# Sixteen experts taken in pairs of 64 places each, with their weights used in plain fp32 as they were loaded

## The chip, the core and the metric

The kernel runs on one core of one Trainium2 chip. The metric is the device time of one execution in microseconds (us); less is better. An execution is one launch with all of its inputs in HBM.

## What is computed

Two transformer blocks run one after the other on 256 tokens of width 1024, everything in float32. The first block is a gated mixer of three branches, a cross attention to 256 memory rows, and a hierarchical mixture of experts; the second is attention with a gated scan, a second cross attention, and a feed-forward layer with a short convolution. Only the mixture of experts changes here:

```python
def hierarchical_moe(h, w_rg, b_rg, w_re, b_re, w_e_gate, w_e_up, w_e_down):
    t = h.reshape(-1, d)                                   # 256 x 1024
    p_grp = softmax(t @ w_rg + b_rg)                       # 4 groups
    g_val, g_idx = top_k(p_grp, 1)
    le = (t @ w_re + b_re).reshape(n, 4, 4)                # 4 experts in each group
    p_exp = softmax(take_along_axis(le, g_idx))
    e_val, e_idx = top_k(p_exp, 2)                         # two experts for a token, of one group
    weight = g_val * e_val / sum(e_val)
    gate = sum(one_hot(g_idx * 4 + e_idx, 16) * weight)    # 256 x 16
    act = silu(t @ w_e_gate[e]) * (t @ w_e_up[e])          # 16 experts, each 1024 -> 256
    return sum over e of (act * gate[:, e]) @ w_e_down[e]  # 256 -> 1024
```

An expert has 2 MiB of gate and up weights and 1 MiB of down weights; the sixteen have 50.3 MB.

## The kernel before

The program is one stream of instructions whose order a planner writes when the kernel is built. Its class `Net` keeps a clock of every engine by a table of costs (`Clock`, `Engine`, `mm`), and small tasks (`spawn`, `advance`, `run`, `need`) are put in where this clock says that their inputs are there.

All weights are one stream, `wstream`, in the order of `PLAN`, cut into pieces of 512 KB (128 partitions by 1024 numbers, `weight_plan`, lines 36 to 108). An expert is six pieces, four of gate and up and two of down. `load` (line 484) issues the DMA of the next piece as soon as a buffer is free: six buffers `stg`, and further ones that `lend` (line 501) takes from the general tiles `t8`, four pieces from before the mixture of experts on (`EARLY`, line 1687) and four more from the experts' loop on (`LEND`, line 1556). They show in the trace as `t<-wstream`.

The precision comes from three F32R matmuls: `split_weight` (line 459) makes of each piece a rounded copy `whi` on ScalarE and the rest `wlo` on VectorE, four and three buffers of a piece each, and the activations are split in the same way. `take` hands out both parts. `mm` (line 659) puts 1 cycle a column on the planner's clock for a matmul of the type F32R, and 4 for plain F32.

The mixture of experts (`moe`, line 1475) goes so. `route` finds for each token its group and counts its rank in the group; `sel` is a 0/1 matrix of 256 tokens by 4 groups by 128 places. While `fill` still computes keys for the second block, `xtok` turns the tokens round, `gathers` collects them by `sel` into 4 x 128 places, split into `xgh` and `xgl`; `scalars` collects the factors of each place and `selt` turns `sel` round. Then all engines read the largest count and pass a branch (line 1552): `overflow` computes what found no place, and it is skipped where no group has more than 128 tokens. A hint for the branch stands in line 1539. `experts` (line 1560) then runs the sixteen experts: for each, 8 chunks by 3 matmuls of 512 columns (`up_mm`), the gated activation (`expert_hidden`: ScalarE, VectorE, two transposes, a split into `mea`), and 2 chunks by 2 halves by 3 matmuls (`down_mm`). The up part of the next expert stands ahead of the down part of this one. All 128 places of a group go through its four experts; after the fourth, `combine` copies the sum from PSUM, splits it, and takes the places back to tokens by 16 matmuls of 256 columns. Then `between` (line 1694) adds the result and begins the second block, whose first weights follow in the stream.

Of the kernel before, what the change touches and what calls it, by code (L numbers as in the profile page):

```python
# [35 lines left out]
def weight_plan():  # L36
# [37 lines left out]
    def gate_up(e):  # L74
        for k in range(0, 8, 2):
            plan.append(("w_e_gu", e, np.arange(k * P, (k + 2) * P), np.arange(512)))

    gate_up(0)
    for e in range(16):
        if e < 15:  # L80
            gate_up(e + 1)
        for k in range(2):
            plan.append(("w_e_down", e, np.arange(k * P, (k + 1) * P), np.arange(1024)))
# [27 lines left out]
PLAN = weight_plan()  # L111

# [158 lines left out]
class Net:  # L271
    BANKS, MORE = 4, 6
    HI, LO, STG = 4, 3, 6
    EARLY, LEND, BACK = 2, 2, 14
# [9 lines left out]
    def __init__(self, ctx, tc, aps, dbg=None):  # L284
# [29 lines left out]
        self.ringed, self.spare, self.lent, self.lending = set(), [], {}, False  # L314

# [115 lines left out]
    def splits(self, margin=None):  # L431

        c, f = self.c, self.c.free
        for n, eng, lim, tag in ((self.n_lo, "dve", self.LO - 1, ("wlo", self.LO)),
# [17 lines left out]

    def room(self, tag, bufs):

        ring = self.rings.get((id(self.wsp), tag), [])
        kept = {x.tensor.name for x in self.kept[tag].values()}
        return 0.0 if len(ring) < bufs else min((self.c.used(x) for x in ring if x not in kept), default=0.0)

    def split_weight(self, eng, n, src):
# [6 lines left out]
        else:  # L466
# [4 lines left out]
            del self.stage[n], src  # L471
            self.ringed.discard(n)
            if n in self.lent:
                view = self.lent.pop(n)
                if self.lending:
                    self.spare.append(view)
            self.load()
# [23 lines left out]
    def lend(self, n):  # L501

        self.lending = True
        for _ in range(n):
            t = self.t8().rearrange("p a t -> p (a t)")
            self.spare += [t[:, :1024], t[:, 1024:]]
        self.load()
# [52 lines left out]
    def force(self):  # L560

        n, eng = (self.n_lo, "dve") if self.n_lo < self.n_hi else (self.n_hi, "act")
# [82 lines left out]

    def block(self, act, k):
# [12 lines left out]
    def mm(self, out, lhsT, rhs, start, stop):  # L659
        n = size(rhs)  # L660
        slow = rhs.dtype == F32
        self.c.issue("pe", max(0.107 if slow else 0.027, 0.0022 + n * (4 if slow else 1) / 2400.0), [lhsT, rhs], [out])
# [301 lines left out]
    def consts(self):  # L964
# [26 lines left out]
        self.iota = c[:, 768:896]  # L991
# [300 lines left out]
    def route(self, rc, sel):  # L1292
# [15 lines left out]
        yield PE  # L1308
        rkp = bank[:, 64:72].rearrange("p (i g) -> p i g", i=2)
        cnt = bank[:, 72:76]  # L1310
        self.mm(rkp[:, 0], self.tri, ohg[:, 0], False, True)
        self.mm(rkp[:, 1], self.ones, ohg[:, 0], False, False)
        self.mm(rkp[:, 1], self.tri, ohg[:, 1], False, True)
        for i in range(2):
            self.mm(cnt, self.ones, ohg[:, i], False, i == 1)
# [14 lines left out]
        rm, rk = self.pc(4), self.pc(1)  # L1330
        V.tensor_mul(rm, rkp, ohg)
        V.tensor_reduce(rk, rm, axis=AX.X, op=ALU.add)
        for g in range(4):
            for i in range(2):
                V.tensor_scalar(sel[:, i, g], self.iota, rk[:, i], ohg[:, i, g:g + 1],
                                op0=ALU.is_equal, op1=ALU.mult)
        self.routed = (ohg, rk)
        yield
# [5 lines left out]
        l2 = self.pc(4)  # L1344
        V.scalar_tensor_tensor(l2, oh1, -3.0e38, ls, op0=ALU.mult, op1=ALU.add)
        _, oh2 = self.first_max(l2)
        V.tensor_add(oh1, oh1, oh2)
# [4 lines left out]
        sv = self.col(16).rearrange("p (i e) -> p i e", i=2)  # L1352
        V.tensor_copy(sv[:, :, 0:1], rc[:, :, None])
        V.tensor_mul(sv[:, :, 1:5], ex, b4(s2))
        self.sv = sv

    def slot_scalars(self, out, bank, sels):

        n = len(sels)
        b = bank[:, :8 * n].rearrange("p (g e) -> p g e", g=n)[:, :, 0:5]  # L1360
        for g, sel in enumerate(sels):
            for i in range(2):
                self.mm(b[:, g], sel[:, i].bitcast(F32), self.sv[:, i, 0:5], i == 0 and g == 0, i == 1)
        self.V.tensor_copy(out[:, :, 0:5], b)
        self.V.tensor_mul(out[:, :, 1:5], out[:, :, 1:5], out[:, :, 0:1].to_broadcast([P, n, 4]))

    def expert_hidden(self, h, sc, e, ea):

        s = self.tile(self.ph[0], [P, T], F32, "hs", 2)
        self.S.activation(s, h[:, 0:T], AF.Silu, scale=sc[:, 0:1])  # L1370
        self.V.scalar_tensor_tensor(s, h[:, T:2 * T], sc[:, 1 + e:2 + e], s, op0=ALU.mult, op1=ALU.mult)
# [4 lines left out]
        hv = h[:, :T].rearrange("p (j t) -> p j t", j=2)  # L1376
        self.S.copy(ea[0], hv)
        self.V.tensor_sub(ea[1], hv, ea[0])

    def new_ea(self, bufs=4):  # L1380
        return [self.tile(self.ph[0], [P, 2, P], F32R, "mea", bufs) for _ in range(2)]

    def up_mm(self, h, xh, xl, wb, k, nk=8):
        for whi, wlo in wb:
            self.mm(h, xh[:, k], whi, k == 0, False)
            self.mm(h, xh[:, k], wlo, False, False)
            self.mm(h, xl[:, k], whi, False, k == nk - 1)
            k += 1
        return k

# [1128 lines left out]
```

## Time and profile before

| | |
|---|---|
| median of 3 runs | 951.21 us (949.74 to 951.82) |
| the profiled execution's own time | 953.05 us |
| its span, first to last instruction | 951.2 us |
| TensorE busy | 924.7 us (97%), 6288 matmul instructions |
| TensorE weight loads | 853.9 us (90%) |
| VectorE busy | 747.1 us (79%) |
| ScalarE busy | 597.7 us (63%) |
| HBM read | 177.72 MB, mean with the rest 188 GB/s over the span |

The profile is that of one execution. Matmuls are pipelined: the duration that a row shows for one contains its way through the array, so what a matmul costs in a stream is read from the distance between two starts and not from its duration. Nearly all instructions were recorded by two helpers, line 266 for VectorE and ScalarE and lines 663 and 667 for TensorE matmuls and transposes, so that groups are told apart by the names of their tiles. A plain fp32 matmul shows as two instructions, each with its own weight load. The stage of the experts begins at 359.04 us and ends at 506.00 us.

### The profile page before, as it was taken

How to read it: one execution, taken by the hardware profiler on the slowest of the kernel's cores; microseconds unless marked ns; L12 is line 12 of the kernel's file. 1: busy time of each engine (PE TensorE's matmuls, PEld its weight loads, DVE VectorE, ACT ScalarE, POOL GpSimd, SP SyncE). 2: the span in 40 equal slices, each digit the busy share in tenths (PEclk: the TensorE clock that was granted, in tenths of full speed). 3: DMA queues.
4: the chain of work that ended last, by engine and by line, in shares of the span. 5: the costliest groups of instructions: out<-in, count | busy, mean ns of one | idle time of the engine just before them, and what ended most of it. 6: DMA issues, size and time to landing. Idle time of an engine off the chain costs nothing.

```text
span 951.2 us, 16270 instructions
## 1 busy us (share of the span) xinstructions
PE 924.7 (97%) x6288; PEld 853.9 (90%) x6288; DVE 747.1 (79%) x1195; ACT 597.7 (63%) x875; POOL 2.3 (0%) x18
## 2 busy tenths in 40 slices
PE   7999999999999999999999999789999899999997
PEld 7999999989989997888888999679998799999995
DVE  5998989767666688989988687968855688888776
ACT  6765444454667658877877479674756566555554
POOL 0000000000000000000000000000000000000000
PEclk8999999999999999999999999999999899999999
DMA  7766646565436739999991445106535356655651
GB/s 278 264 183 193 218 134 214 157 197 180 156 106 190 248 101 348 367 341 338 366 336 37 148 128 184 67 23 186 163 96 199 112 179 198 182 175 176 199 157 45
DMA packets 49906, 179.88 MB, mean 189 GB/s; under 512 B 5664, under 2 KB 5920, under 8 KB 49312
## 3 DMA queue, kind: packets, MB, share of 16 engines
q1 hardware_dynamic: 49824, 178.79, 57.2%
q8 instruction: 51, 0.84, 0.4%
q14 instruction: 31, 0.25, 0.1%
HBM read 177.72 MB, written 1.05 MB: 188 GB/s over the span
## 4 chain that ended last, share of the span: by engine, by line
PE 57%; DVE 3%; ACT 2%; issue 0%; DVEq 0%; ACTq 0%
PE b L663 56%; DVE t L266 2%; ACT t L266 1%; PE b L667 1%; DVE smx L266 0%; ACT prob L266 0%; DVE wlo L266 0%; DVE xT L266 0%; ACT probT L266 0%; DVE prob L266 0%; DVE col L266 0%; ACT whi L266 0%; DVEq L2515 0%; ACT mea L266 0%; DVEq L266 0%
## 5 line engine op out<-in xcount | busy, mean ns | idle before, releaser
L663 PE MATMUL b<-t,whi 128*128 128x256 f32 x2784 | 512.5, 286 | 5.0 <-ACT t L266 4.1
L663 PEld LDWEIGHTS b<-t,whi 128*128 128x128 f32 x2784 | 438.4, 193 | 9.5 <-ACT t L266 4.6
L663 PE MATMUL b<-t,wlo 128*128 128x256 f32 x1392 | 395.4, 284 | 0.0
L266 DVE TENSOR_TENSOR wlo<-stg,whi 128x1024 fp32r<-128x1024 f32 (+1 forms) x269 | 321.1, 1204 | 51.0 <-PE b L663 25.7
L266 ACT CAST whi<-stg 128x1024 fp32r<-128x1024 f32 (+1 forms) x269 | 275.3, 1034 | 119.2 <-PE b L663 85.9
L663 PEld LDWEIGHTS b<-t,wlo 128*128 128x128 f32 x1392 | 268.3, 193 | 0.0
L266 DVE SCALAR_TENSOR_TENSOR t<-pad,vecs,t 128x256 f32<-128x256 f32 x216 | 95.5, 479 | 1.7
L663 PE MATMUL b<-whi,t 128*128 128x512 f32 (+1 forms) x288 | 87.3, 378 | 0.0
L266 DVE TENSOR_TENSOR wlo<-t,whi 128x1024 fp32r<-128x1024 f32 x60 | 71.3, 1220 | 4.6 <-ACT whi L266 1.7
L266 ACT CAST whi<-t 128x1024 fp32r<-128x1024 f32 x60 | 62.7, 1051 | 12.1 <-PE b L663 8.1
L663 PEld LDWEIGHTS b<-whi,t 128*128 128x128 f32 x288 | 52.9, 188 | 8.7
L663 PE MATMUL b<-wlo,t 128*128 128x512 f32 (+1 forms) x144 | 53.8, 373 | 0.2 <-DVE wlo L266 0.2
L266 DVE TENSOR_TENSOR t<-b,t 128x512 fp32r<-128x512 f32 (+1 forms) x38 | 25.6, 687 | 35.6 <-ACT t L266 35.4
L663 PE MATMUL b<-whi,xgh 128*128 128x512 f32 x128 | 51.8, 405 | 1.2 <-ACTq L1552 1.2
L663 PE MATMUL b<-whi,ea 128*128 128x512 f32 x176 | 50.5, 395 | 0.0
L663 PE MATMUL b<-whi,xgl 128*128 128x512 f32 x128 | 50.5, 394 | 0.0
L663 PE MATMUL b<-wlo,xgh 128*128 128x512 f32 x128 | 50.4, 394 | 0.0
L266 ACT ACT_TABLE_LOAD x33 | 42.3, 1283 | 11.3 <-DVE smx L266 7.0
L663 PE MATMUL b<-whi,mea 128*128 128x512 f32 x128 | 42.9, 396 | 0.5 <-ACT mea L266 0.5
L663 PE MATMUL b<-t,t 128*128 128x128 f32 (+1 forms) x224 | 36.0, 313 | 5.3 <-ACT t L266 1.6
L266 ACT ACTIVATE t<-pad,vecs 128x256 f32<-128x256 f32 x52 | 27.7, 587 | 21.4 <-DVE pad L266 21.3
L663 PEld LDWEIGHTS b<-t,t 128*128 128x128 f32 x224 | 31.7, 191 | 9.0 <-ACT t L266 2.5
(218 smaller groups left out, 930.5 us busy)
## 6 DMA issues: line engine op xcount, KB each, us to landing
stg<-wstream SPq DMA_DIRECT2D x259, 512.0 KB, 4.2
t<-wstream SPq DMA_DIRECT2D x60, 512.0 KB, 5.5
t<-memT SPq DMA_DIRECT2D x3, 1024.0 KB, 7.8
stg<-wstream SPq DMA_DIRECT2D x8, 320.0 KB, 3.0
t<-gains SPq DMA_DIRECT2D x1, 1024.0 KB, 7.6
out<-t SPq DMA_DIRECT2D x4, 256.0 KB, 2.0
t<-bands SPq DMA_DIRECT2D x1, 768.0 KB, 5.4
xT<-xT SPq DMA_DIRECT2D x2, 256.0 KB, 5.8
```

Of the source, the lines that this page charges most:

```text
L266: return fn(out, *args, **kw)
L663: self.nc.tensor.matmul(out, lhsT, rhs, start=start, stop=stop, skip_group_check=True)
L667: self.nc.tensor.transpose(out, in_, ident)
```

## The change

- The experts go in eight pairs. Each expert has 64 places of its own, and the 128 columns of a pair lie side by side: the even expert fills partitions 0 to 63 of the PSUM tiles, the odd one 64 to 127. `PLAN` alternates the pieces of the two.
- The experts' pieces are not split. `raw` hands the loaded buffers to plain F32 matmuls with a stationary side of 64 columns and 512 moving columns: 8 chunks for each of two experts up, 2 chunks by 2 halves for each of two experts down, one matmul where there were three. `pass_raw` takes these pieces out of the planner's splitting; the gathered tokens `xg` and the activations `mea` stay whole too.
- The seven buffers of `whi` and `wlo` hold loads in the meantime (`lend_split`, after `fill`).
- `route` ranks the tokens by expert and not by group, which it can do only after the choice of the second expert. `sel` has 16 x 64 columns. The second half of the gathers and all of the turning round of `sel` move into the experts' loop. `combine` comes after each pair, eight times for four.
- The branch asks for more than 64 tokens of an expert; `overflow` is written anew; the hint for the branch is gone.

```diff
-    EARLY, LEND, BACK = 2, 2, 14
+    EARLY, LEND, BACK = 2, 2, 6
...
+    def pass_raw(self):
+
+        if self.n_hi in RAW:
+            self.n_hi = RAW.stop
+        if self.n_lo in RAW:
+            self.n_lo = RAW.stop
...
-        return nk * nc / 1024 * (1.3 if name.startswith("w_e") else 2.7)
+        return nk * nc / 1024 * (0.86 if name.startswith("w_e") else 2.7)
...
+            elif self.borrowed and self.n_dma in RAW:
+                self.lent[self.n_dma] = s = self.borrowed.pop(0)
...
+    def lend_split(self):
+
+        for tag, n in (("whi", self.HI), ("wlo", self.LO)):
+            for _ in range(n):
+                self.borrowed.append(self.tile(self.wsp, [P, 1024], F32, tag, n))
         self.load()
...
+    def raw(self, name, use, count=2):
+
+        ns = range(self.used, self.used + count)
...
+        use([[view(n, c, self.pieces[n][2]) for c in range(self.pieces[n][1])] for n in ns])
+        for n in ns:
+            self.used += 1
+            self.drop(n)
+        self.run()
...
         mg, ohg = self.first_max(l[:, :, 0:4])
-        yield PE
-        rkp = bank[:, 64:72].rearrange("p (i g) -> p i g", i=2)
...
+        _, oh2 = self.first_max(l2)
+        V.tensor_add(oh1, oh1, oh2)
...
+        yield PE
+        rkp = bank[:, 64:96].rearrange("p (i e) -> p i e", i=2)
...
+                V.tensor_tensor(sel[:, i, 8 * half * SLOTS:8 * (half + 1) * SLOTS].rearrange("p (e s) -> p e s", e=8),
+                                self.count1[:, None, :SLOTS].to_broadcast([P, 8, SLOTS]),
+                                self.place[:, i, es, None].to_broadcast([P, 8, SLOTS]), op=ALU.is_equal)
...
-        self.S.copy(ea[0], hv)
-        self.V.tensor_sub(ea[1], hv, ea[0])
+        self.S.copy(ea, h[:, :T].rearrange("p (j t) -> p j t", j=2))
...
-        gd = [self.spawn(gathers(k), 1) for k in range(8)]
-        sct, sT = self.spawn(scalars(), 2), self.spawn(selt(), 3)
+        gd = [self.spawn(gathers(k, 0), 1) for k in range(8)]
         self.warm(AF.Exp)
         self.spawn(self.bounds(), 9)
-        self.tc.mark_branch_hint_location("past", "LikelyTaken", [mybir.EngineType.PE, mybir.EngineType.Activation, mybir.EngineType.DVE, mybir.EngineType.SP])
         fill()
-        self.drain(ro, xt, *gd, sct, sT)
+        self.lend_split()
+        sct = self.spawn(scalars(), 2)
+        self.drain(ro, xt, *gd, sct)
...
-            with self.tc.If(most > P, label="past"):
-                self.overflow(xh, xl, loads, room)
+            with self.tc.If(most > SLOTS, label="past"):
+                self.overflow(loads, room, rc)
...
+            def up(k):
+                def use(ws):
+                    self.settle(ws[0] + ws[1] + [xg[:, k:k + 2, p * P:(p + 1) * P]], [h])
+                    for c in range(2):
+                        for j in range(2):
+                            at = p * P + 64 * j
+                            self.mm(h[half(j)], xg[:, k + c, at:at + 64], ws[j][c], k + c == 0, k + c == 7, 0.5)
+                return use
+
+            for k in range(0, 8, 2):
+                self.raw("w_e_gu", up(k))
+                if p < 2:
+                    late.append(self.spawn(gathers(4 * p + k // 2, 1), 1))
                     self.run()
...
+            if p == 0:
+                selT.append(self.t8(F32R).rearrange("p a t -> p (a t)").rearrange("p (e t) -> p e t", e=8))
+                late.append(self.spawn(selt(selT[0]), 1))
+            y = self.gbanks(2)
...
+            def down(k):
+                def use(ws):
+                    self.settle(ws[0] + ws[1] + [ea[:, k]], y)
+                    for h in range(2):
+                        for j in range(2):
+                            self.mm(y[h][half(j)], ea[:, k, half(j)], ws[j][0][:, h * 512:(h + 1) * 512],
+                                    k == 0, k == 1, 0.5)
+                return use
+
             for k in range(2):
...
+                self.raw("w_e_down", down(k))
+            if p == 0:
+                self.drain(*late)
...
+            last = own[1] = self.spawn(combine(p, y, last), 0)
```

## Rows read from the trace of the kernel before

**Rows 1.** The page, the span in 40 slices of 23.8 us: busy tenths, DMA throughput.
```profile
PE   7999999999999999999999999789999899999997
GB/s 278 264 183 193 218 134 214 157 197 180 156 106 190 248 101 348 367 341 338 366 336 37 148 128 184 67 23 186 163 96 199 112 179 198 182 175 176 199 157 45
```
**Rows 2.** Stretches: us, busy us of five engines (instructions), TensorE clock, DMA share, GB/s.
```profile
359.00:506.00 147.00, 145.90 (x672) 118.88 (x672) 130.21 (x139) 115.76 (x140) 0.00 (x0) 1.00 0.92 343
361.50:375.00 13.50, 13.50 (x62) 10.93 (x61) 12.51 (x14) 11.48 (x14) 0.00 (x0) 1.00 1.02 407
375.00:498.00 123.00, 123.00 (x569) 100.75 (x568) 110.76 (x116) 96.92 (x117) 0.00 (x0) 1.00 0.95 351
```
**Rows 3.** Groups, 359 to 506 us: names, count | busy us, mean ns | idle before, releaser.
```profile
L266 DVE TENSOR_TENSOR wlo<-t,whi 128x1024 fp32r<-128x1024 f32 x54 | 64.2, 1221 | 4.6 <-ACT whi L266 1.7 <-issue 1.4 <-DVEq L1552 1.3
L663 PE MATMUL b<-whi,xgh 128*128 128x512 f32 x128 | 51.8, 405 | 1.2 <-ACTq L1552 1.2
```
**Rows 4.** Waits: SyncE's queue, 358 to 500 us; all engines, 347 to 360 us.
```profile
SPq L514 <- DVE wlo L266: 121.7, 90, 24.4
PE b L663 <- ACTq L1552: 1.2, 1, 1.2
```
**Rows 5.** Timeline of TensorE, the stage's start and end: start, us, names, count [idle before].
```profile
359.04 0.50 PE L663 MATMUL b<-whi,xgh 128*128 128x512 f32 x1 [1.19 <-ACTq L1552]
359.37 0.39 PE L663 MATMUL b<-wlo,xgh 128*128 128x512 f32 x1
...
502.67 0.40 PE L663 MATMUL b<-whi,mea 128*128 128x512 f32 x1
...
504.05 2.05 PE L663 MATMUL b<-selT,t 128*128 128x256 f32 x15 [0.34 <-DVE t L266]
506.00 0.38 PE L663 MATMUL b<-t,whi 128*128 128x256 f32 x1
```
**Rows 6.** Timeline of TensorE elsewhere: plain fp32 matmuls, full width and half width.
```profile
636.93 1.88 PE L663 MATMUL b<-sq,ones 128*128 128x512 f32 x4
...
267.72 1.89 PE L663 MATMUL b<-probT,t 128*128 128x256 f32 x8
...
629.73 1.56 PE L663 MATMUL b<-t,vt 128*128 128x256 f32 x6 [1.03 <-ACT t L266]
631.23 1.09 PE L663 MATMUL b<-probT,vt 128*64 128x256 f32 x8
632.25 0.50 PE L663 MATMUL b<-t,whi 128*128 128x256 f32 x2
```
**Rows 7.** Timeline of TensorE, the gathers and what follows them before the branch.
```profile
347.62 7.62 PE L663 MATMUL b<-sel,t 128*128 128x512 f32 x32
...
356.78 1.07 PE L667 MATMUL b<-cst,sel 128*128 128x128 f32 x8
```
**Rows 8.** Timeline of TensorE, the two transposes of one expert's activation.
```profile
367.97 0.39 PE L663 MATMUL b<-whi,xgl 128*128 128x512 f32 x1
368.20 0.38 PE L667 MATMUL b<-cst,hs 128*128 128x128 f32 x2
...
368.65 0.39 PE L663 MATMUL b<-wlo,xgh 128*128 128x512 f32 x1
```
**Rows 9.** Timeline of VectorE, the writing of sel; its work as the second block begins.
```profile
342.38 2.14 DVE L266 TENSOR_SCALAR sel<-cst,rt,rt 128x128 fp32r<-128x128 f32 x8
...
505.98 0.88 DVE L266 SCALAR_TENSOR_TENSOR t<-xT,gg,t 128x256 fp32r<-128x256 f32 x2 [0.58 <-ACT t L266]
506.78 1.22 DVE L266 TENSOR_TENSOR wlo<-t,whi 128x1024 fp32r<-128x1024 f32 x1
```
**Rows 10.** The page, a DMA queue: packets, MB, share of 16 engines.
```profile
q8 instruction: 51, 0.84, 0.4%
```
**Rows 11.** Stretches, columns as in rows 2, where TensorE's clock falls.
```profile
745.00:750.00 5.00, 2.06 (x12) 1.06 (x10) 3.34 (x11) 2.75 (x10) 0.00 (x0) 0.96 0.36 111
750.00:755.00 5.00, 4.98 (x22) 4.75 (x23) 4.00 (x8) 3.14 (x7) 0.00 (x0) 0.50 0.37 107
```

More of the change, by code (lines that the diff above doesn't have):

```diff
@@ L111 @@
 PLAN = weight_plan()
+RAW = [i for i, p in enumerate(PLAN) if p[0].startswith("w_e")]
+RAW = range(RAW[0], RAW[-1] + 1)
+SLOTS = 64
 VECS = [("norm_mix_g", 8), ("conv_a_w", 124), ("conv_a_b", 4), ("ln_a_g", 4), ("ln_a_b", 4),
@@ L314, in __init__ @@
         self.ringed, self.spare, self.lent, self.lending = set(), [], {}, False
+        self.borrowed = []
     def name(self, s):
@@ L644, in take @@
         return [(hi[:, k * ncol:(k + 1) * ncol], lo[:, k * ncol:(k + 1) * ncol]) for k in range(nk)]
+    def raw(self, name, use, count=2):
+        ns = range(self.used, self.used + count)
+        assert all(self.pieces[n][0] == name for n in ns), name
+        view = lambda n, c, w: self.stage[n][:, c * w:(c + 1) * w]
+        use([[view(n, c, self.pieces[n][2]) for c in range(self.pieces[n][1])] for n in ns])
+        for n in ns:
+            self.used += 1
+            self.drop(n)
+        self.run()
     def block(self, act, k):
@@ L1465, in gather @@
[L1465 to L1473 removed]
+            return s
+        y = [[bank() for _ in range(2)] for _ in range(2)]
@@ new lines, in overflow @@
+        for e in range(16):
+            h = [bank() for _ in range(2)]
+            ups, downs = loads[e]
+            for n, piece in enumerate(ups):
+                s = load(piece)
+                for c in range(2):
+                    k = 2 * n + c
+                    for i in range(2):
+                        self.mm(h[i], xg[:, k, i * P:(i + 1) * P], s[:, c * 512:(c + 1) * 512], k == 0, k == 7)
+            eas = []
+            for i in range(2):
+                eas.append(self.new_ea())
+                for _ in self.expert_hidden(h[i], rc[:, i:i + 1], gm[:, i, e:e + 1], eas[i]):
+                    pass
+            for k in range(2):
+                s = load(downs[k])
+                for i in range(2):
+                    for half in range(2):
+                        self.mm(y[i][half], eas[i][:, k], s[:, half * 512:(half + 1) * 512], e == 0 and k == 0,
+                                e == 15 and k == 1)
@@ L1504, in moe @@
         xt, ro = self.spawn(xtok(), 1), self.spawn(routing(), 0)
-        selT = p.tile([P, 4, T], F32R, name="selT")
-        xgh, xgl = [p.tile([P, 8, 4 * P], F32R, name=n) for n in ("xgh", "xgl")]
+        xg = p.tile([P, 8, 16 * SLOTS], F32, name="xg")
         def scalars():
@@ L1511, in scalars, with selt @@
             b = yield from self.bank()
-            self.slot_scalars(sc, b, [sel[:, :, g] for g in range(4)])
+            self.slot_scalars(sc, b, sel)
             self.unbank(b)
-        def selt():
-            yield from self.wait(ro)
-            for j in range(2):
+        def selt(selT):
+            for j in range(4):
                 b = yield from self.bank()
-                for g in range(2):
+                for n in range(2):
                     for i in range(2):
-                        self.transpose(b[:, g * T + i * P:g * T + (i + 1) * P], sel[:, i, 2 * j + g].bitcast(F32),
+                        c = (2 * j + n) * P
+                        self.transpose(b[:, n * T + i * P:n * T + (i + 1) * P], sel[:, i, c:c + P].bitcast(F32),
@@ L1522, in selt, with gathers @@
                                        self.ident)
                 yield
-                S.copy(selT[:, 2 * j:2 * j + 2], b.rearrange("p (g t) -> p g t", g=2))
+                S.copy(selT[:, 2 * j:2 * j + 2], b.rearrange("p (n t) -> p n t", n=2))
                 self.unbank(b)
-        def gathers(k):
+        def gathers(k, half):
             yield from self.wait(ro, xt)
             b = yield from self.bank()
-            self.gather(b, xh, xl, sel.rearrange("p i g s -> p i (g s)"), k)
+            cs = slice(half * 512, half * 512 + 512)
+            for n, (xp, i) in enumerate([(xp, i) for i in range(2) for xp in xs]):
+                self.mm(b, xp[:, i, k * P:(k + 1) * P], sel[:, i, cs], n == 0, n == 3)
```

273 lines of the change are left out of this document (117 added, 156 removed).

## The prediction

> **What bounds the kernel now.** I read the page first, for the stage: from 357 us on its DMA throughput stands at 336 to 367 GB/s for six slices [rows 1], which is the 50.3 MB of the experts, while TensorE is busy throughout. So two resources look full there, and the other views have to say which one ends last. The stretches do: from 359 to 506 us TensorE is busy for 145.9 of 147.0 us, VectorE for 130.2, ScalarE for 115.8 [rows 2]. The DMA moves 407 GB/s in the first 13.5 us, when all buffers are free, and 351 after that [rows 2]. The waits explain the drop: SyncE's queue waited 121.7 us, in 90 waits, for VectorE to write `wlo`, which frees a load buffer [rows 4]. The loads are held back by the splitting, and the splitting by TensorE's pace, so TensorE is the bound. Its work is five groups like the one shown (128 each of `whi,xgh`, `wlo,xgh`, `whi,xgl` and `whi,mea`, 64 of `wlo,mea`), 576 matmuls of 512 columns [rows 3].
>
> What one costs is read from starts. The 32 gathers of the same shape take 7.62 us, of which 0.39 is the modelled duration of the last [rows 5, 7]: (7.62 - 0.39) / 31 = 0.233 us each, and about 0.16 us of a duration is the way out of the array. 576 x 0.233 = 134.2; four combines of 1.95 (504.05 to 506.00 [rows 5]) are 7.8; the transposes of an expert push the stream back by 0.68 - 2 x 0.233 = 0.22 us [rows 8], sixteen times 3.5. Together 145.5 of the 147.0 us.
>
> **The experts' stage after the change, on TensorE.** It starts at 359.04 us as before, unless the branch says otherwise (below).
> - Plain fp32: four instructions of 512 columns take 1.88 us [rows 6], so a pass is (1.88 - 0.16) / 4 = 0.43 us, and a matmul has two. Full-width ones of 256 columns: eight passes in 1.89 us, 0.216 each. Half-width ones, 64 columns of the array, in the two halves of a tile: eight in 1.09 us [rows 6], 0.116 each. So the two halves ran side by side, four steps of 0.216 and a start of 0.06. That is the very form the change uses. A pair of experts has 24 matmuls (16 up, 8 down), 48 passes, 24 steps of 0.43 = 10.3 us; eight pairs 82.6 us.
> - Eight combines of 1.95: 15.6. They double, since a pair has its own places.
> - Late gathers: 32 x 0.233 = 7.5. They come on top, since the first half takes as long before the branch as all of it did.
> - Turning `sel` round: twice (1.07 - 0.16) [rows 7] = 1.8. Eight times two transposes: 8 x 0.22 = 1.8.
> - The end, from the last matmul into `y` (502.67 + 0.23) to the end of its combine at 506.00, is 3.1 us [rows 5]; less the 1.95 already counted, 1.2.
> - Going from full to half width and back. Six full-width passes from 629.73 would be through at 631.03, the half-width ones start at 631.23; these would be through at 632.10, the next full-width one starts at 632.25 [rows 6]. A round trip costs 0.20 + 0.15 = 0.35 us. I count 8 gathers, 16 halves of combines, 8 transposes and up to 4 of `selT`: 36, of which some will stand next to each other; 30 x 0.34 = 10.2, with 0 and 12.2 as the ends.
>
> Sum: 82.6 + 15.6 + 7.5 + 1.8 + 1.8 + 1.2 + 10.2 = 120.7 us for 147.0. The stage ends at 479.7; it gains 26.3 us.
>
> **What must hide beside it.** The loads: before the branch the DMA is nearly idle (101 GB/s in the slice from 333 to 357 us [rows 1]); with the seven borrowed buffers 6 + 4 + 7 = 17 pieces can be there at the start, 9 us at 407 GB/s for the seven. 79 pieces are left; at 407 GB/s a piece takes 1.29 us, so the last lands near 358 + 102 = 460, at 351 GB/s near 476, and TensorE's last use of one is at 476. So the loads are covered, at the slower rate by nothing. The splits that go (96 of 1.22 us on VectorE [rows 3], as many on ScalarE) were not the bound and give nothing themselves; the second set of combine copies lies in the room they leave.
>
> **Outside the stage.** Routing: the rank now waits for the second choice, about ten small VectorE operations and one turn through TensorE, some 3.5 us in all, and `sel` is the same amount of writing. `sel` was ready at 344.5 and first used at 347.62 [rows 7, 9], so 3.1 us are covered: +0.5 (0 to 2). Between gathers and branch, TensorE loses the 1.07 us of `selT` [rows 7] while VectorE gets four more small operations ahead of the branch: 0. The start of the second block: it found three pieces split, and now its first split comes only as the last expert pieces are used. VectorE then needs about 0.7 + 0.88 + 1.22 us [rows 9] for a piece on which TensorE spends 24 matmuls of half the columns, 24 x 0.12 = 2.9: it just keeps up. +1.5 (0 to 4).
>
> The branch without its hint: TensorE waits 1.2 us there now [rows 4], with the hint. No row shows a branch without one. The nearest price is a block of instructions: 51 packets in 0.4% of 16 engines' span [rows 10], 0.004 x 16 x 951.2 / 51 = 1.2 us each. From 0 to three blocks, 3.6 us; I take two, 2.4, because all engines pass the branch and the slowest counts. The Trainium skill, page "Runtime: NRT & Kernel Launch", section "Instruction fetch mechanics", speaks against the change here: instructions are prefetched in sequence only, and a taken branch with a target outside the window of two pages has to fetch that page before it goes on. It gives no time; the trace of before can't show it, since its branch has the hint.
>
> **The sum.** -26.3 + 0.5 + 1.5 + 2.4 = -21.9 on the profiled execution's 953.05 us: 931.2. That execution lies 1.84 above the median of 951.21, so the median after is about 929.
>
> **Rivals.**
> - *Cheap switches.* The changes of width cost nothing, because the next full-width weights are loaded under the last half-width pass, and the branch costs nothing: 929 - 10.2 - 2.4 = 917. For it: the 0.15 and 0.20 us are seen at two places only, and may have been other waits. Against: both gaps are there with no data to wait for on one side.
> - *The loads bound the stage.* At 351 GB/s, with 17 pieces there, the last lands at 477, and 5 us of use and combine follow: 482, or 931 in all. Were none of the seven there in time, 86 x 1.49 = 128 us of loads end at 487 and the stage at 492: 942. For it: TensorE was never faster than the loads so far. Against: 407 GB/s over 13.5 us with free buffers [rows 2]. The Trainium skill, "DMA: Bandwidth & Descriptors", section "Where 436 GB/s comes from", puts the limit of HBM for a core at about 358 GB/s; by that the last piece would land at 358 + 79 x 1.46 = 474. The trace goes over that limit.
> - *The halves run one after the other.* The other side. The two experts of a pair read different pieces, which land one after the other; if a half that waits for its piece holds back the other, passes are alone in the array. With all alone the 82.6 us double: 929 + 82.6 = 1012, slower. It loses from 21.9 / 82.6 = 27% of the passes on. Against: the half-width rows have two different moving operands too [rows 6], and TensorE, the bound, finds its pieces there.
> - *The branch takes the clock.* After 5 us in which TensorE was busy for 2.06, the granted clock was 0.50 (1.2 GHz) from 750 to 755 us [rows 11]. A wait of 3.6 us at the branch could do the same: some 6 us at half speed, +3: 932. It lies in the range of the forecast.
> - *The skipped part runs.* The change does its work only while no expert has more than 64 tokens. I counted from the reference's inputs: the fullest has 51. Else all sixteen experts follow for all tokens, 16 x 48 passes of 0.43, 330 us more.
>
> **How the numbers follow.** Chances: the forecast 0.63, cheap switches 0.14, the loads 0.09, the clock 0.04, halves in turn 0.06, the skipped part 0.01; 0.03 for a new order of the later stages by the planner, by some 3 us either way. The likeliest gives 929. The range takes in cheap switches, 917, and on the other side 929 + 2 for the last switches, + 1.2 for the branch, + 2.5 for the late splits, + 1.5 for routing, + 3 for the clock, and the worse loads: 942; halves in turn and the tails are left out, under 2 in 10. Faster by over 0.2% (about what a measurement of this kernel can tell from no change) 0.90, within it 0.02, slower 0.08.
>
> **What would show it.** Half-width `xg` matmuls in steps of 0.43 us for two, and the last at about 476 us. Few waits of TensorE for DMA; SyncE's queue waits for TensorE and no longer for `wlo`. Gaps of 0.15 to 0.20 us around gathers and combines. A gap of 2 to 4 us at the branch with instruction packets in it. The second block begins near 482, with TensorE waiting for a split once or twice. I am wrong if steps are 0.86, if TensorE waits for DMA through the stage, or if the later stages grow by what this one gains.

## The result and the profile after

| | before | after |
|---|---|---|
| median | 951.16 us (4 runs, 949.74 to 951.82) | 930.11 us (4 runs, 929.52 to 931.17) |
| ratio | | 0.9782, 95% interval 0.9765 to 0.9799 |
| profiled execution, own time / span | 953.05 / 951.2 us | 929.52 / 927.7 us |
| experts' stage on TensorE | 359.04 to 506.00: 147.0 us | 358.37 to 482.51: 124.1 us |
| from the stage's end to the last instruction | 445.2 us | 445.2 us |

The change saves 21.05 us between the medians and 23.5 us between the two profiled executions. In the profiles 22.8 us of it lie in the one stage, and 0.67 in its earlier start. The forecast was 929 us, with a range from 917 to 942.

First the page of after, DMA throughput in 40 slices of 23.2 us (before: [rows 1]):

```profile
GB/s 294 257 186 184 224 141 203 170 182 183 180 94 180 254 176 282 359 380 409 409 363 47 119 117 216 5 63 165 182 94 206 129 187 176 190 182 177 186 158 45
```

Two slices at 409 GB/s stand where before had none above 367. The stretches of after say what is busy in the stage (us, busy us and instructions of TensorE, its weight loads, VectorE, ScalarE, GpSimd, then granted clock, DMA share, GB/s; before: [rows 2]):

```profile
358.30:482.50 124.20, 121.68 (x576) 50.71 (x576) 20.51 (x33) 24.04 (x45) 0.00 (x0) 0.98 1.00 384
400.00:470.00 70.00, 70.00 (x346) 27.86 (x343) 9.81 (x16) 10.92 (x22) 0.00 (x0) 1.00 1.02 405
```

VectorE went from 130.2 busy us to 20.5 and ScalarE from 115.8 to 24.0. TensorE is still busy nearly throughout, with 576 instructions for 672: 384 half-width passes where 576 matmuls were, and 192 of gathers, combines and transposes. The waits of SyncE's queue and of TensorE in and around the stage (engine, line, what it waited for: us, times, longest; before: [rows 4]):

```profile
SPq L544 <- PE b L706: 43.5, 32, 2.9
SPq L544 <- DVE wlo L271: 26.2, 1, 26.2
...
PE b L706 <- DVE t L271: 2.3, 3, 1.7
PE b L706 <- PEq L1575: 2.3, 1, 2.3
```

A load buffer is now freed by TensorE itself. The one long wait for a `wlo` begins at 477 us, when the experts' loads are all issued, and belongs to the second block. TensorE waited for data once at length, 1.7 us, and 2.3 us at the branch. Both are seen in its timeline (start, us, names, count, [idle before and what ended it]; before: [rows 5]):

```profile
354.25 1.84 PE L706 MATMUL b<-svs,sel 128*128 128x10 f32 x16
358.37 3.68 PE L706 MATMUL b<-t,xg 128*64 128x512 f32 x8 [2.27 <-PEq L1575]
361.98 1.77 PE L706 MATMUL b<-sel,t 128*128 128x512 f32 x4
363.68 1.94 PE L706 MATMUL b<-t,xg 128*64 128x512 f32 x8
365.55 1.19 PE L706 MATMUL b<-sel,t 128*128 128x512 f32 x4
366.66 1.94 PE L706 MATMUL b<-stg,xg 128*64 128x512 f32 x8
...
410.21 1.94 PE L706 MATMUL b<-wlo,xg 128*64 128x512 f32 x8
411.98 1.89 PE L706 MATMUL b<-t,xg 128*64 128x512 f32 x8
413.70 1.89 PE L706 MATMUL b<-t,mea 128*64 128x512 f32 x8
415.52 0.44 PE L710 MATMUL b<-cst,hs 128*128 128x128 f32 x2
...
475.86 1.89 PE L706 MATMUL b<-whi,mea 128*64 128x512 f32 x8
...
478.37 1.22 PE L706 MATMUL b<-t,t 128*128 128x256 f32 x8 [0.32 <-DVE t L271]
481.24 1.09 PE L706 MATMUL b<-t,t 128*128 128x256 f32 x7 [1.65 <-DVE t L271]
482.51 1.10 PE L706 MATMUL b<-t,whi 128*128 128x256 f32 x2 [0.18 <-ACT t L271]
```

Read it by starts. From 410.21 to 415.52 three groups of eight passes run through: 5.31 us for 24 passes, which is 12 steps of 0.43 = 5.16 and 0.15 for the entry from full width. Eight passes between two full-width blocks take 365.55 - 363.68 = 1.87 = 4 x 0.43 + 0.15, and the four gathers behind them 366.66 - 365.55 = 1.11, which is 0.93 by [rows 7] and 0.18 for the way back to full width. But the first eight passes took 361.98 - 358.37 = 3.61 us and the first gathers 1.70. There TensorE had half its clock (columns as above):

```profile
356.00:357.00 1.00, 0.10 (x1) 0.01 (x1) 0.77 (x5) 0.14 (x1) 0.00 (x0) 0.70 0.66 61
357.00:358.00 1.00, 0.00 (x0) 0.00 (x0) 0.97 (x3) 0.00 (x0) 0.00 (x0) 0.50 0.63 246
358.00:363.00 5.00, 4.63 (x11) 1.70 (x12) 0.00 (x0) 0.00 (x0) 0.00 (x0) 0.50 0.98 342
363.00:364.00 1.00, 1.00 (x5) 0.50 (x5) 0.00 (x0) 0.21 (x1) 0.00 (x0) 0.89 0.63 229
```

The granted clock was at its lower level, 1.2 GHz, from 356.4 to 363.2 us: it fell 0.3 us into the gap at the branch, behind the 16 short matmuls of `svs,sel`. It cost (3.61 - 1.87) + (1.70 - 1.11) = 2.3 us.

### The profile page after: what moved, and what is told of

Read it like the earlier page. It is cut to its first block, busy times and chain, and to the rows that moved or that the text cites. A ratio compares the mean times of both kernels' runs of the same rounds, so it can differ in the third digit from the quotient of the medians.

```text
span 927.7 us, 15588 instructions
## 1 busy us (share of the span) xinstructions
PE 901.5 (97%) x6184; PEld 786.6 (85%) x6184; DVE 633.8 (68%) x1086; ACT 500.6 (54%) x773; POOL 2.1 (0%) x18
## 4 chain that ended last, share of the span: by engine, by line
PE 56%; DVE 3%; ACT 1%; DMA 1%; issue 0%; DVEq 0%; ACTq 0%
PE b L706 55%; DVE t L271 2%; ACT t L271 1%; PE b L710 1%; DMA stg<-wstream 1%; DVE wlo L271 0%; DVE smx L271 0%; ACT probT L271 0%; DVE col L271 0%; DVE xT L271 0%; DVEq L2562 0%; DVE prob L271 0%; DVE gg L271 0%; ACTq L271 0%; DVEq L271 0%
## 5 line engine op out<-in xcount | busy, mean ns | idle before, releaser
L271 DVE TENSOR_TENSOR wlo<-stg,whi 128x1024 fp32r<-128x1024 f32 (+2 forms) x225 | 268.8, 1201 | 50.5 <-PE b L706 25.7
L271 ACT CAST whi<-stg 128x1024 fp32r<-128x1024 f32 (+2 forms) x225 | 229.2, 1030 | 112.2 <-PE b L706 79.8
L271 DVE TENSOR_TENSOR t<-b,t 128x512 fp32r<-128x512 f32 (+1 forms) x46 | 31.4, 688 | 63.3 <-ACT t L271 62.6
L706 PEld LDWEIGHTS b<-t,t 128*128 128x128 f32 x352 | 49.6, 196 | 21.1 <-issue 10.9
L706 PE MATMUL b<-t,t 128*128 128x256 f32 (+1 forms) x352 | 57.2, 313 | 5.1 <-DVE t L271 2.9
L271 DVE SCALAR_TENSOR_TENSOR hs<-b,sc,hs 128x256 f32<-128x256 f32 x8 | 3.9, 482 | 50.9 <-ACT hs L271 50.9
L706 PEld LDWEIGHTS b<-whi,ea 128*128 128x128 f32 x176 | 32.4, 188 | 7.2
L271 DVE TENSOR_TENSOR t<-t,t 128x512 f32<-128x512 f32 (+4 forms) x46 | 29.3, 663 | 12.3 <-ACT t L271 10.1
L271 ACT CAST t<-b 128x512 fp32r<-128x512 f32 x34 | 19.5, 588 | 29.6 <-PE b L706 23.4
L706 PEld LDWEIGHTS b<-wlo,t 128*128 128x128 f32 x144 | 27.1, 188 | 5.0 <-DVE wlo L271 0.8
```

What stands on the lines that cost most here:

```text
L271: return fn(out, *args, **kw)
L706: self.nc.tensor.matmul(out, lhsT, rhs, start=start, stop=stop, skip_group_check=True)
```

## The experiments

The theory under test (A in the texts): TensorE's passes bound the stage, two halves run side by side, each change of width costs, and the loads are covered. Each diff is against the changed kernel.

**The hint put back.**

```diff
+        self.tc.mark_branch_hint_location("past", "LikelyTaken", [mybir.EngineType.PE, mybir.EngineType.Activation, mybir.EngineType.DVE, mybir.EngineType.SP])
         fill()
```

> The changed kernel with the branch hint of the kernel before put back. Theory A, the missing hint costs twice, in TensorE's wait at the branch (2.27 us there in the changed kernel, in which TensorE's own branch took 3.5 us) and in the clock that falls to 1.2 GHz from 356.4 to 363.2 us: the wait falls to 1.0 to 1.6 us, the clock stays at 2.4 GHz, the first step of eight half-width passes takes 1.87 us instead of 3.61, and the total falls by 2.3 to 3.5 us to about 927. Theory B, VectorE passes the branch last anyway and the hint is worth nothing: the wait stays above 2 us, the clock falls all the same, total 930.

926.31 us (924.94 to 927.69, 5 runs), ratio to before 0.9749 (0.9735 to 0.9762). Its timeline at the branch:

```profile
356.51 1.94 PE L706 MATMUL b<-t,xg 128*64 128x512 f32 x8 [1.02 <-PEq L1576]
358.38 1.20 PE L706 MATMUL b<-sel,t 128*128 128x512 f32 x4
```

The gap is 1.02 us in place of 2.27, and the clock did not fall: the first step is 1.87 us. The stage takes 356.51 to 478.34, 121.8 us, and the difference to 124.1 is just the 2.3 us of the clock. Is the fall the doing of the missing hint? **The same program once more** was to say so.

> The kernel of e1_hint once more. In e1_hint's profiled execution the granted clock stayed at 1.00 behind the branch, in those of e8_best and e11_hinttrips, which have the hint too, it fell to 0.50 for some 3 us. If the fall belongs to the kernel, it is absent here too: the first step of 8 passes takes 1.87 us, and the median is again 926.3 us (924.9 to 927.7). If it belongs to the single execution, a fall of 1 to 2.3 us may show here, and the hint's own share of e1_hint's 3.8 us is the 1.25 us by which TensorE's gap became shorter plus the part of the falls that the shorter gap prevents.

927.04 us (925.20 to 930.53, 5 runs), ratio 0.9738 (0.9715 to 0.9761). Its profiled execution was the slowest of the five, 930.53:

```profile
358.23 3.68 PE L706 MATMUL b<-t,xg 128*64 128x512 f32 x8 [1.59 <-PEq L1576]
361.83 2.08 PE L706 MATMUL b<-sel,t 128*128 128x512 f32 x4
```

One program, two executions, 5.6 us apart: the gap was 1.02 and 1.59 us, the clock stayed up in one and fell from 357 to 364 in the other. So the fall belongs to the single execution, and my first reading, that the hint prevents it, does not hold. What holds is the median: 926.3 and 927.0 with the hint against 930.1 without, some 3.1 to 3.8 us, of which the shorter gap shows 0.7 to 1.25 us in the two traces. The runs' mean granted clocks point to the rest: 0.988 over the ten executions with the hint, 0.9855 over the four without, and 0.0026 of 928 us is 2.4 us, an estimate for all falls of the clock in an execution and not only the one at the branch. How often it falls there with the hint and how often without isn't settled.

**No two halves side by side.** Every expert matmul runs over all 128 columns, so that each half's passes are alone in the array.

```diff
-  self.mm(h[half(j)], xg[:, k + c, at:at + 64], ws[j][c], k + c == 0, k + c == 7, 0.5)
+  self.mm(h, xg[:, k + c, p * P:(p + 1) * P], ws[j][c], k + c == 0 and j == 0, k + c == 7 and j == 1)
...
-  self.mm(y[h][half(j)], ea[:, k, half(j)], ws[j][0][:, h * 512:(h + 1) * 512], k == 0, k == 1, 0.5)
+  self.mm(y[h], ea[:, k], ws[j][0][:, h * 512:(h + 1) * 512], k == 0 and j == 0, k == 1 and j == 1)
```

> The changed kernel with every expert matmul over all 128 columns of a pair instead of its own 64 (both experts' weights are applied to all places of the pair and added up, so the experts are not kept apart). The number of passes, the loads and the copies stay; only the running side by side is taken away. Theory A, the two halves ran side by side and TensorE is the bound: 384 passes of 0.43 us that were hidden show up, less the 30 round trips between widths of 0.33: +165.1 - 82.6 - 9.9 = +72.7, about 1003 us. Theory B, the loads bound the stage (they run at 408 GB/s from 405 us on): part of this is hidden and the total grows by clearly less, to under 990.

1001.55 us (1 run). Its timeline and its stage:

```profile
440.49 3.60 PE L706 MATMUL b<-t,xg 128*128 128x512 f32 x8
443.93 3.60 PE L706 MATMUL b<-t,mea 128*128 128x512 f32 x8
```

```profile
358.80:554.90 196.10, 194.59 (x576) 98.36 (x576) 20.70 (x32) 24.04 (x45) 0.00 (x0) 0.99 0.74 248
```

Eight passes take 443.93 - 440.49 = 3.44 us, eight half-width ones 1.72 (411.98 to 413.70 above). The stage grows by 196.1 - 124.1 = 72.0 us: the passes' 82.6 a second time, less the changes of width (30 x 0.33 = 9.9), would be 72.7. With 248 GB/s moved, the loads had nothing to do with it. Taking the experts side by side is worth more than the whole gain; without it the change would have lost some 50 us.

**The order of the halves.** The two passes over one half stand next to each other in the program, not those of the two halves.

```diff
-                    for c in range(2):
-                        for j in range(2):
+                    for j in range(2):
+                        for c in range(2):
...
-                    for h in range(2):
-                        for j in range(2):
+                    for j in range(2):
+                        for h in range(2):
```

> The changed kernel with the two halves' matmuls not alternating: within a step first the two of the even expert, then the two of the odd one. Theory A, each half of the array takes its own next matmul, whatever stands between (as the half-width rows of the second block suggest, where one half's four instructions also stand ahead of the other's): total within 1 us of 930, steps of 1.87 us. Theory B, they overlap only where neighbours in the program belong to different halves: three of four passes of a half run alone, a step takes about 3 us, and the total grows by 50 us or more.

931.69 us (1 run), the eight passes again 1.87 us apart from the next block (362.68 to 364.56):

```profile
362.68 1.94 PE L706 MATMUL b<-t,xg 128*64 128x512 f32 x8
364.56 1.19 PE L706 MATMUL b<-sel,t 128*128 128x512 f32 x4
```

The order hardly matters to the passes: theory B's 50 us are out, and blocks of 16 or 24 passes are 0.05 us longer. The total is 1.6 us above the changed kernel's where theory A allowed 1. At the stage's end the combines now wait for ScalarE twice, 0.7 to 0.8 us each, which they did not before.

**No borrowed buffers.** The seven tiles of `whi` and `wlo` hold no loads.

```diff
-        for tag, n in (("whi", self.HI), ("wlo", self.LO)):
-            for _ in range(n):
-                self.borrowed.append(self.tile(self.wsp, [P, 1024], F32, tag, n))
         self.load()
```

> The changed kernel without the seven borrowed buffers (the free split tiles stay unused), so that 10 pieces and not 17 can be loaded ahead of the branch and 14 and not 21 be held. Theory A, TensorE is the bound and the loads are covered with room: total 930 to 932. Theory B, the loads are the bound, or so near that the seven pieces ahead of the branch are what covers them: each is 1.28 us at 408 GB/s, total 935 to 939, with TensorE waiting for DMA in the later part of the stage.

931.92 us (929.71 to 933.03, 4 runs), ratio 0.9806 (0.9791 to 0.9821). In its profile the clock did not fall at the branch, and up to 448 us every block of matmuls takes the same time as in the changed kernel, 2.4 us earlier. Then four of them grow, by 0.50, 1.16, 0.78 and 0.32 us, 2.8 in all; two of these are here, with the DMA in the same time:

```profile
463.11 3.65 PE L703 MATMUL b<-t,xg 128*64 128x512 f32 x16
466.59 2.67 PE L703 MATMUL b<-stg,mea 128*64 128x512 f32 x8
469.19 0.44 PE L707 MATMUL b<-cst,hs 128*128 128x128 f32 x2
469.56 2.26 PE L703 MATMUL b<-stg,mea 128*64 128x512 f32 x8
471.75 0.39 PE L703 MATMUL b<-t,t 128*128 128x256 f32 x1
```

```profile
440.00:470.00 30.00, 29.91 (x137) 12.42 (x138) 3.73 (x6) 4.38 (x9) 0.00 (x0) 1.00 1.03 409
```

The 24 passes from 463.11 to 469.19 take 6.08 us in place of 5.30. The loads bind from 448 to 472 us when the seven pieces are not there at the stage's start. The total, 1.8 us above the changed kernel's and in theory A's range, does not tell this by itself, since the clock at the branch did not fall here. So the loads are covered, but by the borrowed buffers, and by little.

**Fewer changes of width.** A combine is one block of 16, and the late gathers go two at a time.

```diff
-                if p < 2:
-                    late.append(self.spawn(gathers(4 * p + k // 2, 1), 1))
+                if p < 2 and k % 4 == 2:
+                    for n in range(2):
+                        late.append(self.spawn(gathers(4 * p + k // 2 - 1 + n, 1), 1))
...
-                if m % 4 == 0:
+                if m == 0:
```

> The changed kernel with fewer changes of width on TensorE, and the same passes: a pair's combine is one block of 16 instead of two of 8, and the late gathers run two at a time: some 12 round trips between half and full width go of 30. Theory A (a round trip costs 0.33 us wherever it stands): up to 4 us less, 926 to 927.5 us, less what the combine then waits for the second half of y. Rival (the 0.33 us is the first weight load after any wait, or is hidden by other limits such as the loads): 929.5 to 931 us.

925.67 us (924.30 to 927.80, 5 runs), ratio 0.9732 (0.9716 to 0.9748): 4.4 us less than the changed kernel.

```profile
358.27 5.35 PE L706 MATMUL b<-t,xg 128*64 128x512 f32 x16 [2.49 <-PEq L1575]
363.55 2.13 PE L706 MATMUL b<-sel,t 128*128 128x512 f32 x8
...
402.20 1.89 PE L706 MATMUL b<-whi,xg 128*64 128x512 f32 x8
404.01 2.18 PE L706 MATMUL b<-t,t 128*128 128x256 f32 x16
406.12 0.64 PE L706 MATMUL b<-whi,xg 128*64 128x512 f32 x1
```

A combine takes 406.12 - 404.01 = 2.11 us; its halves took 1.14 each, apart. In the trace of the stage there are 21 stretches of half-width passes in place of 30. Nine round trips of 0.33 are 3.0 us, and the clock's fall at the branch cost 1.7 here (363.55 - 358.27 = 5.28 us for 16 passes that take 3.58 at the higher clock) for 2.3: together the 3.6 us by which the stage is shorter (358.27 to 478.76). So not all of the 4.4 us is width. I had counted on twelve round trips.

**The split work given back.** Of all that the change took from the two other engines, is any a gain by itself?

```diff
         for n in ns:
+            hi, lo = [self.tile(self.ph[0], [P, 640], mybir.dt.bfloat16, t, 1) for t in ("dhi", "dlo")]
+            self.S.copy(hi, self.cst[:, :640])
+            self.V.tensor_sub(lo, self.cst[:, :640], hi)
             self.used += 1
```

> The changed kernel with ScalarE and VectorE given back some five eighths of the work that the change took from them in the expert stage: for each of the 96 loaded pieces one copy and one subtraction of 640 columns, out of a constant into scratch that nobody reads, so that no buffer is held by it: about 0.7 us x 96 = 67 us of ScalarE and 0.8 us x 96 = 77 us of VectorE in a stage of 124 us. Theory A (TensorE's passes set the stage, the splits lay beside it): 929 to 933 us, the excess from the short steps between a pair's up and down passes, which queue behind this work. Rival (taking the splits off the two engines gave a part of the gain itself): 940 us or more.

984.15 us, 54 us above the changed kernel: in the rival's range, but for a reason that neither side had foreseen. The waits show a flaw of the experiment:

```profile
DVE dlo L271 <- ACT dhi L271: 75.6, 93, 1.2
ACT dhi L271 <- DVE dlo L271: 75.3, 85, 0.9
...
PE b L713 <- DVE hs L271: 48.2, 6, 15.2
```

With one `hi` for all, ScalarE waits for VectorE and VectorE for ScalarE at every piece; the pair needs 1.6 us for each of 96, 155 us in a stage of 124, and TensorE waited for the gated activation behind that queue. It says nothing on the question. With the subtraction reading constants alone (`self.V.tensor_sub(lo, self.cst[:, :640], self.cst[:, 128:768])`) the two engines are independent:

> As e7_work, with the flaw of that run mended: there VectorE's subtraction read ScalarE's scratch, and one scratch buffer made the two engines take turns, 0.79 + 0.82 us a piece, 155 us in all. Here the 96 copies on ScalarE (0.72 us each, 70 us) and the 96 subtractions on VectorE (0.82 us each, 79 us) read constants alone and wait for nothing of each other. Theory A (TensorE's passes set the stage): 930 to 935 us, the excess from short steps that queue behind this work. Rival (free VectorE and ScalarE were themselves a part of the gain): 940 us or more.

929.89 us (929.00 to 931.68, 4 runs), ratio 0.9765 (0.9750 to 0.9780). Its groups on VectorE and ScalarE, and its stage:

```profile
L271 DVE TENSOR_TENSOR dlo<-cst 128x640 bf16<-128x640 f32 x96 | 79.0, 823 | 2.9 <-PEq L1578 0.4
```

```profile
L271 ACT CAST dhi<-cst 128x640 bf16<-128x640 f32 x96 | 69.7, 726 | 4.5 <-PEq L1578 2.2
```

```profile
359.60:484.60 125.00, 122.17 (x576) 50.76 (x576) 97.13 (x128) 89.71 (x141) 0.00 (x0) 0.98 1.00 387
```

79 us more on VectorE and 70 more on ScalarE cost nothing that can be measured. The removed splits gave nothing by themselves.

**The end of the stage.** TensorE's wait of 1.65 us at 481.24 is for VectorE, whose timeline in the changed kernel shows why:

```profile
477.63 0.69 DVE L271 TENSOR_TENSOR t<-b,t 128x512 fp32r<-128x512 f32 x1 [4.78 <-ACT t L271]
478.24 2.35 DVE L271 TENSOR_TENSOR wlo<-t,whi 128x1024 fp32r<-128x1024 f32 x2
480.50 0.68 DVE L271 TENSOR_TENSOR t<-b,t 128x512 fp32r<-128x512 f32 x1
...
481.18 0.68 DVE L271 TENSOR_TENSOR xT<-xT,b 128x512 f32<-128x512 f32 x1
```

Two splits for the second block stand ahead of the second copy of `y`. They were held back until both copies are issued:

```diff
         self.pass_raw()
+        if self.nosplit:
+            return False
...
+            self.nosplit = p == 7
             for k in range(2):
                 self.raw("w_e_down", down(k))
...
                 V.tensor_sub(yt[:, 1, cs], y[j], yt[:, 0, cs])
                 yield
+            self.nosplit = False
```

> The changed kernel with one order changed: no split of the second block's weights is placed between the last pair's last passes and the two copies of its y, so that VectorE's second y copy comes ahead of the two splits of 2.35 us. Theory A (the two splits stand in the chain of the stage's end): the second y copy moves from 480.50 to about 478.8, TensorE's wait of 1.65 us on it goes, and the second block's first matmul comes 1.0 to 1.7 us earlier; the fall of the granted clock after it may go too: 927.5 to 929.2 us. Rival (the splits are needed by the second block's first matmuls, so that these wait for them in place of the y copy): within 0.4 us of the changed kernel's 930.1.

929.36 us (928.70 to 931.07, 5 runs), ratio 0.9771 (0.9758 to 0.9784), not to be told from the changed kernel:

```profile
475.24 1.89 PE L708 MATMUL b<-whi,mea 128*64 128x512 f32 x8
...
477.75 2.05 PE L708 MATMUL b<-t,t 128*128 128x256 f32 x15 [0.32 <-DVE t L271]
482.42 1.10 PE L708 MATMUL b<-t,whi 128*128 128x256 f32 x2 [2.62 <-ACT t L271]
```

The wait for `y` is gone, and one of 2.62 us takes its place one step later: the splits now stand ahead of VectorE's addition to `x`, on which the second block's first activation hangs. So theory A's gain did not come. What the rival foresaw came in another form, for it is not the matmuls themselves that wait for these splits, and 929.36 lies between the two ranges.

**Put together.** The hint, fewer changes of width, and the splits held back (e8_best in the texts):

> The changed kernel with three edits together: the hint for the branch kept, the combine in one block with the late gathers in twos, and the splits of the second block held until the last y is copied. If the three are independent: 3.8 us (hint, measured) + up to 4 (width changes) + 1.0 to 1.7 (order at the end) less than 930.1, so 921 to 923.5 us. If the loads take over as the bound once TensorE is faster: not under 925 us, with TensorE's waits for DMA in the last third of the stage.

923.80 us (921.17 to 925.90, 5 runs), ratio 0.9708 (0.9690 to 0.9726), 0.3 us above the range for three independent gains. And without the last of the three:

> The changed kernel with two edits of e8_best and not the third: the hint for the branch, and fewer changes of width; the splits of the second block stand where the changed kernel puts them. If the two are independent: 930.1 - 3.8 (hint, e1_hint) - 4.4 (width changes, e6_trips) = 921.9 us, below e8_best's 923.8, and holding the splits costs time. If the granted clock at the branch is what the hint's gain hung on, and it falls here as it did in e8_best: 923 to 924.5 us.

923.58 us (922.32 to 924.96, 5 runs), ratio 0.9702 (0.9688 to 0.9717). Holding the splits is worth nothing here either, and the hint gives 2.1 us on top of the fewer changes of width, less than its 3.1 to 3.8 alone. The gap at the branch was 0.30 and 0.35 us, and still the clock fell behind it in both profiled executions: the first 16 passes took 5.3 us for 3.58. Lastly, in the version with all three only one split was let in ahead of the addition to `x`:

> e8_best with the order at the stage's end changed again: between the last pair's copies of y and VectorE's first addition to x only one split of the second block's weights is placed, not two; the second stands behind that addition. In e8_best TensorE waited 2.61 us there, for a t of ScalarE that followed that addition. Theory A (that wait is VectorE's second split): 0.8 to 1.2 us less than e8_best's 923.8, so 922.6 to 923.0. Rival (the second split is then what the second block's first matmuls wait for): within 0.4 us of 923.8.

930.08 us (929.11 to 931.58, 5 runs), ratio 0.9774 (0.9760 to 0.9787): 6 us lost, which neither side had foreseen. The step itself did what it should: TensorE's wait at the stage's end fell from 2.61 to 1.48 us, and the second block began at 474.01. The planner had then written another order for what follows, and 50 us later stands a wait that e8_best does not have:

```profile
525.06 3.08 PE L711 MATMUL b<-rk,t 64*128 64x256 f32 x16 [4.04 <-DVE rk L271]
```

From the second block's first matmul to the end it needed 453 us, e8_best 444; this wait is 4 of the 9, and the rest was not taken apart. The best version of the study is the changed kernel with the hint and the fewer changes of width, 6.5 us (0.7%) below it; e8_best, 0.2 us behind, can't be told from it.

## Why the prediction was right, point by point

**The bound, right.** TensorE was the bound and stayed it. Giving VectorE and ScalarE 149 us of work back moved nothing; making every pass run alone lengthened the stage by 72 us.

**The passes, right.** 24 steps of 0.43 us for a pair, as read from the few half-width rows of before [rows 6]: 5.31 us for 24 passes. The rival of halves in turn (1012) is out: the run that makes them so gave 1001.55, about the rival's price less the changes of width, which that run hasn't, and its steps are those that the changed kernel does not show.

**The changes of width, right.** 30 were forecast at 0.34 us; the trace has 30 stretches of half-width passes, at 0.15 into half width and 0.18 out of it (forecast 0.20 and 0.15), and taking nine of them away gave what nine cost. The cheap-switch rival (917) is out. The Trainium skill, page "TensorEngine Tiling (Array Packing)", says that a change of the tiling mode drains the array, without a time; the runs agree that a change costs, 0.33 us for both ways, and do not show what the time consists of.

**The stage as a whole.** Forecast 120.7 us, measured 124.1. The 2.3 us of the clock and the wait of 1.65 us for the second `y`, which the forecast carried outside the stage, leave 120.2: the terms of the sum were 0.5 us too large together.

**The loads, right.** I had the last piece land between 460 us (at 407 GB/s) and 476 (at 351), the time of its last use, so that at the slower rate nothing was left. The DMA moved 405 GB/s over 70 us of the stage, near the faster end. Without the borrowed buffers the loads did bind, for 2.8 us at the end, so the loads' rival (931 to 942) names a limit that is near, though in this kernel it does not decide. The limit of 358 GB/s that the Trainium skill names for a core ("DMA: Bandwidth & Descriptors", "Where 436 GB/s comes from") is passed here for 70 us on end.

**The branch and what stands ahead of it, mis-sized twice.** The terms were +2.4 for the branch and +0.5 for the routing, and 0 for the `selT` that goes. TensorE's gap grew by 2.27 - 1.19 = 1.08 us, and `selT` came off with about as much, so that these two cancel. Yet the stage began 0.67 us earlier than before where I had it 2.9 later. The gathers ahead of it began 0.83 earlier (346.79 for 347.62), so that the longer routing was covered; but 0.58 of this stands 10 us after the program's start (the same matmul at 9.26 for 9.84), ahead of all that the change touches, and in the other runs' profiles the gathers begin at 346.2 to 348.0 us. So the 0.8 belongs to the two executions, and not to the change. The price of two instruction blocks, 1.2 us each, was too high: with the hint the gap was 0.30 to 1.59 us, without it 2.2 to 2.5, so that its whole price is 2.2 or less. It was also the wrong stand-in: the gap was to have instruction packets in it, and the queue of [rows 10] moved none from 356 to 358.5 us, while in the kernel before, with the hint, it moved one in the same 2.5 us. What TensorE's sequencer waits for in the gap stays open. Then the clock fell and took 2.3 us back. I had that as a rival with a chance of 0.04; it came in most profiled executions, and by luck it makes the sum look so exact. The Trainium skill's rule that a taken branch breaks the sequential prefetch ("Runtime: NRT & Kernel Launch", "Instruction fetch mechanics") agrees in sign alone: without the hint the gap is longer, but the fetch that it speaks of is not seen in the gap of 2.27 us.

**The late splits, right in size, wrong in place.** +1.5 was forecast, as TensorE waiting for a split in the second block. What came was 1.65 us of waiting for `y`, behind two splits in VectorE's queue. Moving both showed that the term stands for VectorE's work, not for one order: it comes back one step later. Moving one of them past the addition did shorten the wait, to 1.48 us, but that version lost more behind it.

**The second block, right.** It takes 445.2 us in both. At its start the clock fell once more in after (0.59 from 482 to 486 us), 1.2 us. It came back at the program's place where before has its own fall (0.96 and 0.50 [rows 11], then 0.85 from 755 to 760 us), because after falls there too, but for half as long (0.85 from 725 to 730 and 0.81 from 730 to 735). A third fall in after, 0.77 from 585 to 600 us, cost nothing that lasted: matmul for matmul, after lags by 1.2 us ahead of it and by 1.1 behind it. That the two blocks come out equal is luck too.

In the sum: -22.8 for the stage with its clock and the wait in it, -0.67 for its earlier start, 0 behind it, make the 23.5 us between the profiles. The forecast's -21.9 is 1.6 too small: +3.6 for branch, routing and `selT` (0.8 of it the executions' own), -2.3 for the clock, and +0.3 from the rest. That the median still lies 1.1 above the forecast comes from the profiled executions, before's 1.9 above its median and after's 0.6 below.

## What to carry to other kernels

Price small shared-array matmuls by starts, and count the changes of width between blocks: here 30 of 0.33 us were 10 us, and grouping nine of them away was the cheapest gain left. When an engine's work is removed, ask first whether that engine was the bound, and whether what it held (here seven tiles) can carry loads in the meantime: the freed tiles were worth 2.8 us of the stage, the freed engines nothing. A profile shows one execution: two of the same program lay 5.6 us apart here, at mean granted clocks of 0.992 and 0.985, so a gain read from a clock in one trace is to be held against the medians.

## What the runs showed of the hardware that was not expected

- The granted clock fell to half at the branch or just behind it in ten of the fourteen profiled executions, and not in the other four: the kernel before, the one without borrowed buffers, the last of those put together, and one of the two executions with the hint alone. The gap of TensorE at the branch was 0.30 to 2.5 us where it fell and 0.30 to 2.2 us where it didn't, so the gap's length does not decide it. In all of them 16 matmuls of 5 or 10 columns stand ahead of it. What decides stays open; no run tried to fill the gap with work.
- The half-width passes run side by side even if the two halves do not alternate in the program one by one: 1.87 us for eight in either order.
- The DMA moved 405 GB/s for 70 us while TensorE was busy throughout, a rate that before had reached only for 13.5 us (407 [rows 2]), and far above its 351.
